# Matrix passes of 272, 256 and 264 columns in place of three of 264, on tiles whose blocks are 1152 or 1024 bytes apart

## The chip, the cores and the metric

One core of a Trainium2 chip runs the whole program; the other cores are idle. The metric is the device time of one execution in microseconds (us). Three executions of the kernel before took 2701.05, 2701.96 and 2702.11 us, median 2701.96.

## What is computed

One decoder layer for 256 prompt tokens and 8 decode tokens (one for each of 8 requests) that share the weights. In float32:

```
x = x + 1/2 * SwiGLU_1(RMSNorm(x))
h = RMSNorm(x);  one input projection h @ w_in
A = retention (8 heads; the prompt in chunks, the decode tokens from a state)
B = sparse attention (an indexer picks keys; 16 query heads, 4 key heads)
x = x + (sigmoid(g_A) * (A @ w_ret_out) + sigmoid(g_B) * (B @ w_att_out)) @ w_o
x = x + 1/2 * SwiGLU_2(RMSNorm(x))
```

The model width is 2048 and the FFN's 5632. All weights are read once, 512 KB for each half block of them. Nearly all arithmetic is in the products of the 264 tokens with the weights.

## The kernel before

The activations lie transposed: features on the 128 partitions, tokens along the columns, prompt tokens in columns 0 to 255 and decode tokens in 256 to 263 (T = TP + NB = 256 + 8). Sixteen blocks of 128 features make the model width.

Products with weights run on TensorE in a float32 form that reads rounded operands (F32R), so each operand is split into a rounded high part and the rest, the low part. `mblock` (L236) makes one output block of 128 features: it loads weights by SyncE's queue in two transfers of eight 128x128 blocks, rounds them on ScalarE (`wh`, L247), subtracts on VectorE or GpSimd (`wl`, L248), and for each 128 rows of the contraction runs three passes over all 264 tokens (below called a block of passes): `wh` with the high part (L251), `wh` with the low part (L252), `wl` with the high part (L253). Each pass is one weight load and one matmul, and all add into one PSUM tile `ps`; three such tiles exist. `Norm.add` (L280) and `split` (L301) make the high parts (ScalarE) and low parts (VectorE) of the activations.

High and low parts, x, and most other large tiles come from one pool, `qpool`, of NQ = 23 buffers of 4224 bytes a partition. `quad` (L146) takes a buffer, `Blocks` (L167) hands out its four blocks of 264 floats, 1056 bytes apart.

`ffn` (L305) runs in three chunks of the 5632 features: gate and up products, the SwiGLU product `h`, its split, then the second weight's products, added into x. Between the two FFNs stand the input projections (`mixblock`, one `mblock` each, in the order of L49: indexer, retention, attention, gates). Their evacuations are interleaved with generators that do everything else: `step` (L414) runs pieces of the queues a, b and c after each block, and `drain` empties them. Queue c holds `retention_prompt`, then `retention_decode` (L888: 16 steps, each takes three buffers, `sb`, `kq` and `kv`), then `group_norm` (L956). Queue b holds the decode indexer, then `decode_attention` (L786: eight requests in two half steps each; a request takes `kb`, a half step `qb` and two `pr`). Each half step's products run on GpSimd (L802, L905), the reductions on VectorE (L804, L906). The final order of each engine's instructions is found by the tile framework's scheduler from priorities; `ahead()` raises them. On each engine instructions run in that order.

The work on the path: `norm` and FFN1 (0 to 790 us), the projections with their generators (790 to 1640 us), the three output projections (to 1940 us), FFN2 (to the end).

Of the kernel before, what the change touches and what calls it, by code (L numbers as in the profile page):

```python
# [23 lines left out]
NB = 8  # L24
T = TP + NB
FF = 5632
FB = FF // P
# [23 lines left out]

NQ = 23
AHEAD = 1500
# [68 lines left out]
def layer(ctx: ExitStack, tc: tile.TileContext, xT, gains, consts, dmat, didx, pt, state, cidx, ck, cv,  # L122
# [22 lines left out]

    def quad(dt=F32, shape=(P, 4, T), s="q"):  # L146
        return qpool.tile(list(shape), dt, tag="q", name=nm(s))
# [19 lines left out]
    class Blocks:  # L167
# [3 lines left out]
        def __getitem__(self, i):  # L171
# [3 lines left out]
            return self.t[q][:, i % 4, :]  # L175

    warm = cpool.tile([P, 1], F32, name="warm")
    nc.vector.memset(warm, 0.0)
# [26 lines left out]
    nc.vector.memset(ones1, 1.0)  # L205
    onesw = cpool.tile([P, SW], F32, name="onesw")
    nc.vector.memset(onesw, 1.0)
# [27 lines left out]

    def mblock(src, nk, hi, lo, m=P):  # L236
        ps = psm.tile([P, 512], F32, tag="ps", name=nm("ps"))
        for c0 in range(0, nk, 8):
            n = min(8, nk - c0)
            wr = rawp.tile([P, 8, P], F32, tag="wr", name=nm("wr"))  # L240
            wh = hip.tile([P, 8, P], F32R, tag="wh", name=nm("wh"))
            wl = lop.tile([P, 8, P], F32R, tag="wl", name=nm("wl"))
            lo_turn[0] += 1
            eng = nc.gpsimd if lo_turn[0] % 4 in lo_pool[0] else nc.vector
            with ahead():
                nc.sync.dma_start(wr[:, :n, :m], src[:, c0:c0 + n, :])
                nc.scalar.activation(wh[:, :n, :m], wr[:, :n, :m], AF.Copy)  # L247
                eng.tensor_sub(wl[:, :n, :m], wr[:, :n, :m], wh[:, :n, :m])  # L248
            for k in range(n):
                g = c0 + k  # L250
                nc.tensor.matmul(ps[:m, :T], wh[:, k, :m], hi[g], start=g == 0, stop=False)  # L251
                nc.tensor.matmul(ps[:m, :T], wh[:, k, :m], lo[g], start=False, stop=False)  # L252
                nc.tensor.matmul(ps[:m, :T], wl[:, k, :m], hi[g], start=False, stop=g == nk - 1)  # L253
        return ps[:m, :T]
# [10 lines left out]
    def rsqrt(src, y, ms, t):  # L265
        """y = (src + EPS) ** -0.5"""
        nc.vector.tensor_scalar(ms, src, EPS, None, op0=ALU.add)
        root(ms, y, t)
        newton(y, ms, t)

    class Norm:
        """Gains and sums of squares of the blocks of x as they come; the mean's root follows at the evacuations."""

        def __init__(self, gain):
            self.gain = cc(gain)
            self.hi = Blocks(KB, F32R, "hi")
            self.lo = Blocks(KB, F32R, "lo")
            self.acc = wt("acc", tag="acc", bufs=2)

        def add(self, k, x):  # L280
            g = self.gain[:, k:k + 1]
            nc.scalar.activation(self.hi[k], x, AF.Copy, scale=g)  # L282
            nc.vector.scalar_tensor_tensor(self.lo[k], x, g, self.hi[k], op0=ALU.mult, op1=ALU.subtract)  # L283

# [15 lines left out]

    def split(v, hi, lo):  # L301
        nc.scalar.activation(hi, v, AF.Copy)
        nc.vector.tensor_sub(lo, v, hi)

    def ffn(norm, w1, w2, out, early=0):  # L305
        for ci, (j0, j1) in enumerate(CHUNKS):
            n = j1 - j0
            hh, hl = Blocks(n, F32R, "hh"), Blocks(n, F32R, "hl")
            for j in range(j0, j1):
                pg = mblock(w1[2 * j], KB, norm.hi, norm.lo)  # L310
                if j < early:
                    c = wt("c")
                    nc.scalar.activation(c, pg, AF.Copy)
                    pg = c
                if j == 0:
                    rstd = norm.done()
                g = wt("g")
                nc.vector.tensor_mul(g, pg, rstd)
                s = wt("s")
                nc.scalar.activation(s, g, AF.Silu)  # L320
                s2 = wt("s2")
                nc.gpsimd.tensor_mul(s2, s, rstd)  # L322
                pu = mblock(w1[2 * j + 1], KB, norm.hi, norm.lo)
                if j < early - 1:
                    c = wt("c")
                    nc.scalar.activation(c, pu, AF.Copy)
                    pu = c
                h = wt("h")
                nc.vector.tensor_mul(h, pu, s2)  # L329
                split(h, hh[j - j0], hl[j - j0])  # L330
            for m in range(KB):
                ps = mblock(w2[m][:, j0:j1, :], n, hh, hl)
                out(m, ps, ci == len(CHUNKS) - 1)
# [32 lines left out]
    def mixblock(src, m=P):  # L366
        return mblock(src, KB, mixn.hi, mixn.lo, m)

# [284 lines left out]
    def rms_roots(sums):  # L653
        """Steps from functions that give PSUM sums to the tiles of two roots each."""
        ss, y, t = (mt(n, (P, 2, T)) for n in ("ss", "y", "t"))
        for j, f in enumerate(sums):
            pq = aux()
            f(pq[:, :T])
            nc.scalar.activation(ss[:, j, :], pq[:, :T], AF.Identity, bias=epst)
        yield  # L660
        root(ss, y, t)
        yield
        newton(y, ss, t)
        yield y
# [210 lines left out]
    def bcast_rows(src, which, scale=1.0):  # L875
        """src [128 d, (b, h)] as rows of d in DRAM, to be read onto all partitions."""
        n = src.shape[1]
# [198 lines left out]
    lo_pool[0] = (0,)  # L1076
    RHI, RLO = Blocks(16, F32R, "rhi"), Blocks(16, F32R, "rlo")
    for i in range(16):
# [6 lines left out]
        nc.gpsimd.tensor_mul(r, s, RO[i])  # L1085
        split(r, RHI[i], RLO[i])
        step(b=1)
    drain("b")

    MG = Blocks(16, s="mg")  # L1090
    AHI, ALO = Blocks(16, F32R, "ahi"), Blocks(16, F32R, "alo")
    MHI, MLO = Blocks(16, F32R, "mhi"), Blocks(16, F32R, "mlo")

# [10 lines left out]
    for m in range(KB):  # L1104
        ps = mblock(wro[m], 16, RHI, RLO)
        nc.vector.tensor_mul(MG[m], ps, sgate(0, m))
        split(ATT[m], AHI[m], ALO[m])
    for m in range(KB):
        ps = mblock(wao[m], 16, AHI, ALO)
        t = wt("at")  # L1110
        nc.vector.tensor_mul(t, ps, sgate(1, m))
        t2 = wt("at2")
        nc.gpsimd.tensor_add(t2, t, MG[m])
        split(t2, MHI[m], MLO[m])

# [6 lines left out]
    for m in range(KB):  # L1122
        ps = mblock(wo[m], 16, MHI, MLO)
        nc.vector.tensor_add(X[m], ps, X[m])
# [79 lines left out]
```

## Time and profile before

| | us |
|---|---|
| median of three runs | 2701.96 |
| the profiled execution, its span from first to last instruction | 2703.1 |
| TensorE busy | 2621.5 (97%) |
| VectorE busy | 1596.6 (59%) |
| ScalarE busy | 1163.4 (43%) |
| GpSimd busy | 647.2 (24%) |

The profiled execution is known by its span alone. PE is TensorE, PEld its weight loads (which overlap the matmuls), DVE is VectorE, ACT ScalarE, POOL GpSimd, SP SyncE; a q behind a name is that engine's sequencer or its issue of a DMA. Matmuls are pipelined: the duration of one is its latency, and the time between the starts of two is what it costs. Names such as ps<-hi,wh say what an instruction writes and reads; L252 is line 252 of the kernel.

### The profile page before, as it was taken

How to read it: one execution, taken by the hardware profiler on the slowest of the kernel's cores; microseconds unless marked ns; L12 is line 12 of the kernel's file. 1: busy time of each engine (PE TensorE's matmuls, PEld its weight loads, DVE VectorE, ACT ScalarE, POOL GpSimd, SP SyncE). 2: the span in 40 equal slices, each digit the busy share in tenths (PEclk: the TensorE clock that was granted, in tenths of full speed). 3: DMA queues.
4: the chain of work that ended last, by engine and by line, in shares of the span. 5: the costliest groups of instructions: out<-in, count | busy, mean ns of one | idle time of the engine just before them, and what ended most of it. 6: DMA issues, size and time to landing. Idle time of an engine off the chain costs nothing.

```text
span 2703.1 us, 51188 instructions
## 1 busy us (share of the span) xinstructions
PE 2621.5 (97%) x21205; PEld 2588.8 (96%) x21205; DVE 1596.6 (59%) x2301; ACT 1163.4 (43%) x1551; POOL 647.2 (24%) x427
## 2 busy tenths in 40 slices
PE   7999999999999899999988899999999999999999
PEld 7999999999999699899988899999999999999999
DVE  6555555555566578568798845566655555554554
ACT  5443344334453333443545654444544334433443
POOL 3110011001127443445455543231111001100110
PEclk9999999999999899998998999999999999999999
DMA  6556555655566354468886666666555655566555
GB/s 216 180 181 184 181 180 181 184 182 180 173 218 214 108 170 157 141 213 282 266 291 228 203 195 223 206 208 210 180 181 182 181 183 180 180 181 183 181 166 173
DMA packets 164745, 520.67 MB, mean 193 GB/s; under 512 B 21680, under 2 KB 38640, under 8 KB 164512
## 3 DMA queue, kind: packets, MB, share of 16 engines
q1 hardware_dynamic: 126496, 445.31, 52.4%
q10 hardware_dynamic: 32112, 56.51, 6.4%
q0 software_dynamic: 5904, 15.59, 1.8%
q8 instruction: 166, 2.72, 0.4%
q14 instruction: 67, 0.55, 0.1%
HBM read 495.73 MB, written 21.60 MB: 191 GB/s over the span
## 4 chain that ended last, share of the span: by engine, by line
PE 82%; DVE 7%; issue 3%; DMA 3%; POOL 2%; ACT 2%; ACTq 0%; DVEq 0%; POOLq 0%
PE ps L252 27%; PE ps L251 26%; PE ps L253 26%; DVE wl L248 2%; DMA wr<-win 1%; POOL wl L248 1%; POOL pr L802 1%; DVE junk L534 1%; ACT wh L247 1%; DMA qb<-rows 0%; DMA kq<-rows 0%; DMA vb<-cv,rowi 0%; DVE sTs L804 0%; PE aux L443 0%; DVE sb L903 0%
## 5 line engine op out<-in xcount | busy, mean ns | idle before, releaser
L247 ACT ACTIVATE wh<-wr 128x1024 fp32r<-128x1024 f32 x866 | 902.0, 1043 | 1294.1 <-PE ps L252 838.5
L248 DVE TENSOR_TENSOR wl<-wr,wh 128x1024 fp32r<-128x1024 f32 (+2 forms) x798 | 990.3, 1241 | 740.2 <-ACT wh L247 739.1
L251 PE MATMUL ps<-hi,wh 128*128 128x264 f32 x4624 | 1326.4, 287 | 19.3 <-ACT hi L282 10.1
L253 PE MATMUL ps<-hi,wl 128*128 128x264 f32 x4624 | 1326.7, 287 | 16.2 <-DVE wl L248 13.3
L252 PE MATMUL ps<-lo,wh 128*128 128x264 f32 x4624 | 1329.2, 287 | 1.6 <-DVE lo L283 1.5
L251 PEld LDWEIGHTS ps<-hi,wh 128*128 128x128 f32 x4624 | 878.0, 190 | 23.0 <-ACT hi L282 10.1
L253 PEld LDWEIGHTS ps<-hi,wl 128*128 128x128 f32 x4624 | 876.1, 189 | 24.6 <-DVE wl L248 16.1
L252 PEld LDWEIGHTS ps<-lo,wh 128*128 128x128 f32 x4624 | 877.0, 190 | 8.7 <-issue 5.3
L322 POOL TENSOR_TENSOR s<-s,rstd 128x264 f32<-128x264 f32 x88 | 127.5, 1449 | 1252.6 <-ACT s L320 1252.6
L253 PE MATMUL ps<-hh,wl 128*128 128x264 f32 x1408 | 399.0, 283 | 0.0
L252 PE MATMUL ps<-hl,wh 128*128 128x264 f32 x1408 | 398.7, 283 | 0.0
L251 PE MATMUL ps<-hh,wh 128*128 128x264 f32 x1408 | 398.5, 283 | 0.0
L252 PEld LDWEIGHTS ps<-hl,wh 128*128 128x128 f32 x1408 | 264.7, 188 | 0.0
L251 PEld LDWEIGHTS ps<-hh,wh 128*128 128x128 f32 x1408 | 264.6, 188 | 0.0
L253 PEld LDWEIGHTS ps<-hh,wl 128*128 128x128 f32 x1408 | 264.4, 188 | 0.0
L248 POOL TENSOR_TENSOR wl<-wr,wh 128x1024 fp32r<-128x1024 f32 x68 | 170.2, 2508 | 289.9 <-ACT wh L247 250.4
L802 POOL TENSOR_TENSOR pr<-qb,kb 128x1024 f32<-128x1024 f32 x32 | 93.4, 2937 | 57.9 <-DMA qb<-rows 23.5
L291 POOL TENSOR_TENSOR acc<-acc,sq 128x264 f32<-128x264 f32 x45 | 40.5, 900 | 153.7 <-ACT sq L290 152.7
L329 DVE TENSOR_TENSOR h<-ps,s 128x264 f32<-128x264 f32 x88 | 38.0, 432 | 66.0 <-PE ps L253 62.7
L362 POOL DMA_INDIRECT kt<-cidx,kix x64 | 71.9, 1123 | 19.1 <-issue 18.5
L252 PE MATMUL ps<-mlo,wh 128*128 128x264 f32 x256 | 72.9, 285 | 0.0
L252 PE MATMUL ps<-alo,wh 128*128 128x264 f32 x256 | 72.7, 284 | 0.0
(311 smaller groups left out, 2270.0 us busy)
## 6 DMA issues: line engine op xcount, KB each, us to landing
wr<-win SPq DMA_DIRECT2D x224, 512.0 KB, 4.4
wr<-w1a SPq DMA_DIRECT2D x176, 512.0 KB, 3.8
wr<-w1b SPq DMA_DIRECT2D x176, 512.0 KB, 3.7
wr<-w2a SPq DMA_DIRECT2D x80, 512.0 KB, 3.7
wr<-w2b SPq DMA_DIRECT2D x80, 512.0 KB, 3.6
wr<-wro SPq DMA_DIRECT2D x32, 512.0 KB, 4.8
wr<-wao SPq DMA_DIRECT2D x32, 512.0 KB, 4.9
wr<-wo SPq DMA_DIRECT2D x32, 512.0 KB, 3.9
```

The lines of the kernel that those rows point to most:

```text
L247: nc.scalar.activation(wh[:, :n, :m], wr[:, :n, :m], AF.Copy)
L248: eng.tensor_sub(wl[:, :n, :m], wr[:, :n, :m], wh[:, :n, :m])
L251: nc.tensor.matmul(ps[:m, :T], wh[:, k, :m], hi[g], start=g == 0, stop=False)
L252: nc.tensor.matmul(ps[:m, :T], wh[:, k, :m], lo[g], start=False, stop=False)
L253: nc.tensor.matmul(ps[:m, :T], wl[:, k, :m], hi[g], start=False, stop=g == nk - 1)
L291: nc.gpsimd.tensor_add(self.acc, self.acc, sq)
L322: nc.gpsimd.tensor_mul(s2, s, rstd)
L329: nc.vector.tensor_mul(h, pu, s2)
L362: nc.gpsimd.indirect_dma_start(out=KT[p][pg // 8][:, o:o + PG], out_offset=None, in_=cidx, in_offset=bass.IndirectOffsetOnAxis(ap=kix[:, p ...
L534: nc.vector.scalar_tensor_tensor(junk, VS, thr, onesw, op0=ALU.is_ge, op1=ALU.mult, accum_out=out)
L802: nc.gpsimd.tensor_mul(pr, qb, k.to_broadcast([P, 2, 4, P]))
```

## The change

Three passes over 264, 264 and 264 columns become passes over 272, 256 and 264. The low parts of the eight decode tokens are stored right behind the high parts of all 264 tokens in the same block, so that the pass of `wh` over the wide block (272 columns, TW = T + NB) gives the high products of all tokens and, in eight more columns of PSUM, the low products of the decode tokens. The low parts of the prompt have a tile of their own, 256 floats a block. After the last pass ScalarE copies the eight extra columns out of PSUM, and VectorE adds them to columns 256 to 263.

```diff
-NQ = 23
+NQ = 21
+TW = T + NB
+TS = 288
...
+    class Pair:
...
+                self.t[q] = (qpool.tile([P, 4, TS], F32R, tag="q", name=nm(self.s + "h")),
+                             qpool.tile([P, 4, TP], F32R, tag="q", name=nm(self.s + "l")))
...
+        def hi(self, i):
+            return self.tiles(i)[0][:, i % 4, :T]
+        def wide(self, i):
+            return self.tiles(i)[0][:, i % 4, :TW]
+        def lod(self, i):
+            return self.tiles(i)[0][:, i % 4, T:TW]
+        def lop(self, i):
+            return self.tiles(i)[1][:, i % 4, :]
...
-                nc.tensor.matmul(ps[:m, :T], wh[:, k, :m], hi[g], start=g == 0, stop=False)
-                nc.tensor.matmul(ps[:m, :T], wh[:, k, :m], lo[g], start=False, stop=False)
-                nc.tensor.matmul(ps[:m, :T], wl[:, k, :m], hi[g], start=False, stop=g == nk - 1)
+                nc.tensor.matmul(ps[:m, :TW], wh[:, k, :m], x.wide(g), start=g == 0, stop=False)
+                nc.tensor.matmul(ps[:m, :TP], wh[:, k, :m], x.lop(g), start=False, stop=False)
+                nc.tensor.matmul(ps[:m, :T], wl[:, k, :m], x.hi(g), start=False, stop=g == nk - 1)
+        d = st([P, NB], tag="lod", bufs=4)
+        nc.scalar.activation(d[:m], ps[:m, T:TW], AF.Copy)
+        nc.vector.tensor_add(ps[:m, TP:T], ps[:m, TP:T], d[:m])
...
-    def split(v, hi, lo):
+    def split(v, x, i):
+        hi = x.hi(i)
         nc.scalar.activation(hi, v, AF.Copy)
-        nc.vector.tensor_sub(lo, v, hi)
+        for lo, c in ((x.lop(i), slice(0, TP)), (x.lod(i), slice(TP, T))):
+            nc.vector.tensor_sub(lo, v[:, c], hi[:, c])
```

`Norm.add` makes its low parts in the same two pieces. A buffer of the pool is now 4 x 288 floats, 4608 bytes; `quad` takes one of that size and gives views of 264 columns at a distance of 1152 bytes, so x, too, is loaded and stored in rows of 1056 bytes. The pool has 21 buffers. A constant, `onesw`, gets 16 more floats, which moves the pool behind it by 64 bytes: every block of the high and of the prompt's low parts now starts on a multiple of 128 bytes. In the kernel before, 1056 bytes being eight and a quarter times 128, one block in four did.

The order of each engine shows where the sizes and the new instructions stand. On TensorE, in the second chunk of FFN1, before (ps is the output block, hi and lo the norm's parts, wh and wl the weights'):

```order
L251 MATMUL ps_4268<-hi_138,wh_4270 128x264
L252 MATMUL ps_4268<-lo_140,wh_4270 128x264
L253 MATMUL ps_4268<-hi_138,wl_4271 128x264
L251 MATMUL ps_4268<-hi_148,wh_4300 128x264
L252 MATMUL ps_4268<-lo_150,wh_4300 128x264
L253 MATMUL ps_4268<-hi_148,wl_4301 128x264
```

and now (nh and nl are the norm's high and low tiles):

```order
L282 MATMUL ps_4493<-nh_142,wh_4495 128x272
L283 MATMUL ps_4493<-nl_143,wh_4495 128x256
L284 MATMUL ps_4493<-nh_142,wl_4496 128x264
L282 MATMUL ps_4493<-nh_156,wh_4525 128x272
L283 MATMUL ps_4493<-nl_157,wh_4525 128x256
L284 MATMUL ps_4493<-nh_156,wl_4526 128x264
```

The order is the same, and the columns differ.

On VectorE in the first chunk of FFN1, before (h is the SwiGLU product, hh and hl its parts, g the scaled gate):

```order
L329 TENSOR_TENSOR h_1814<-ps_1753,s_248_1751 128x264
L248 TENSOR_TENSOR wl_1918<-wr_1916,wh_1917 128x1024
L303 TENSOR_TENSOR hl_1419<-h_1814,hh_1418 128x264
L248 TENSOR_TENSOR wl_1955<-wr_1953,wh_1954 128x1024
L318 TENSOR_TENSOR g_1879<-ps_1818,rstd_282 128x264
```

and now:

```order
L287 TENSOR_TENSOR ps_1710<-ps_1710,lod_1771 128x8
L366 TENSOR_TENSOR h_1774<-ps_1710,s_251_1708 128x264
L279 TENSOR_TENSOR wl_1921<-wr_1919,wh_1920 128x1024
L340 TENSOR_TENSOR hl_1497<-h_1774,hh_1496 128x256
L340 TENSOR_TENSOR hh_1496<-h_1774,hh_1496 128x8
L279 TENSOR_TENSOR wl_1951<-wr_1949,wh_1950 128x1024
L287 TENSOR_TENSOR ps_1779<-ps_1779,lod_1840 128x8
L355 TENSOR_TENSOR g_1843<-ps_1779,rstd_301 128x264
```

Ahead of each reader of an output block stands the add of eight columns, and a split is two subtractions.

On GpSimd, among the gate projections, where retention_decode (kv) and decode_attention (pr) run, before:

```order
L802 TENSOR_TENSOR pr_14880<-qb_14878,kb_14875 128x1024
L802 TENSOR_TENSOR pr_14883<-qb_14878,kb_14875 128x1024
L802 TENSOR_TENSOR pr_15049<-qb_15047,kb_14875 128x1024
L905 TENSOR_TENSOR kv_14891<-sb_14886,kq_14888 128x1024
L802 TENSOR_TENSOR pr_15052<-qb_15047,kb_14875 128x1024
L782 DMA kb_15145<-ck,rowi_12896 128x512 x2
L802 TENSOR_TENSOR pr_15150<-qb_15148,kb_15145 128x1024
L905 TENSOR_TENSOR kv_15060<-sb_15055,kq_15057 128x1024
L802 TENSOR_TENSOR pr_15153<-qb_15148,kb_15145 128x1024
L905 TENSOR_TENSOR kv_15240<-sb_15235,kq_15237 128x1024
L802 TENSOR_TENSOR pr_15330<-qb_15328,kb_15145 128x1024
```

and now:

```order
L839 TENSOR_TENSOR pr_15571<-qb_15569,kb_15566 128x1024
L839 TENSOR_TENSOR pr_15574<-qb_15569,kb_15566 128x1024
L942 TENSOR_TENSOR kv_15582<-sb_15577,kq_15579 128x1024
L839 TENSOR_TENSOR pr_15746<-qb_15744,kb_15566 128x1024
L839 TENSOR_TENSOR pr_15749<-qb_15744,kb_15566 128x1024
L819 DMA kb_15845<-ck,rowi_13515 128x512 x2
L942 TENSOR_TENSOR kv_15757<-sb_15752,kq_15754 128x1024
L839 TENSOR_TENSOR pr_15850<-qb_15848,kb_15845 128x1024
L839 TENSOR_TENSOR pr_15853<-qb_15848,kb_15845 128x1024
L942 TENSOR_TENSOR kv_15943<-sb_15938,kq_15940 128x1024
L839 TENSOR_TENSOR pr_16036<-qb_16034,kb_15845 128x1024
```

Before, a product of the one stream stood between the two products of a half step of the other, and the next keys kb were gathered early; now a half step's two products stand together, and the streams take turns.

## Rows read from the trace of the kernel before

**Rows 1.** The page, part 1: busy us of each engine, share of the span, instructions.

```profile
PE 2621.5 (97%) x21205; PEld 2588.8 (96%) x21205; DVE 1596.6 (59%) x2301; ACT 1163.4 (43%) x1551; POOL 647.2 (24%) x427
```

**Rows 2.** The page, part 4: the chain of waits, shares by engine.

```profile
PE 82%; DVE 7%; issue 3%; DMA 3%; POOL 2%; ACT 2%; ACTq 0%; DVEq 0%; POOLq 0%
```

**Rows 3.** The page, part 5: passes on the two largest kinds of moving tile; busy us, mean ns.

```profile
L251 PE MATMUL ps<-hi,wh 128*128 128x264 f32 x4624 | 1326.4, 287 | 19.3 <-ACT hi L282 10.1
...
L251 PE MATMUL ps<-hh,wh 128*128 128x264 f32 x1408 | 398.5, 283 | 0.0
```

**Rows 4.** Busy time by stretch, FFN1 and FFN2: us, each engine (instructions), PEclk, DMA, GB/s.

```profile
50.00:150.00 100.00, 100.00 (x828) 100.00 (x827) 52.22 (x60) 42.21 (x52) 13.34 (x9) 1.00 0.59 184
...
2200.00:2400.00 200.00, 200.00 (x1647) 200.00 (x1647) 104.42 (x119) 82.18 (x101) 23.76 (x16) 1.00 0.57 181
```

**Rows 5.** Timeline of TensorE in FFN1, first passes of blocks: start us, us, instruction.

```profile
100.37 0.28 PE L251 MATMUL ps<-hi,wh 128*128 128x264 f32 x1
...
100.72 0.28 PE L251 MATMUL ps<-hi,wh 128*128 128x264 f32 x1
...
101.09 0.28 PE L251 MATMUL ps<-hi,wh 128*128 128x264 f32 x1
...
101.82 0.28 PE L251 MATMUL ps<-hi,wh 128*128 128x264 f32 x1
```

**Rows 6.** Busy time by stretch, after a wait of TensorE in the middle.

```profile
1459.00:1465.00 6.00, 6.00 (x29) 6.00 (x30) 6.00 (x10) 3.56 (x8) 0.01 (x1) 0.54 0.91 285
```

**Rows 7.** Timeline of TensorE there: first passes after the wait.

```profile
1458.91 0.59 PE L251 MATMUL ps<-hi,wh 128*128 128x264 f32 x1 [6.74 <-DVE g L984]
...
1459.52 0.42 PE L253 MATMUL ps<-hi,wl 128*128 128x264 f32 x1
1459.74 0.42 PE L251 MATMUL ps<-hi,wh 128*128 128x264 f32 x1
```

**Rows 8.** Timeline of TensorE in FFN2, first passes of blocks.

```profile
2050.15 0.28 PE L251 MATMUL ps<-hi,wh 128*128 128x264 f32 x1
...
2050.89 0.28 PE L251 MATMUL ps<-hi,wh 128*128 128x264 f32 x1
...
2051.61 0.28 PE L251 MATMUL ps<-hi,wh 128*128 128x264 f32 x1
```

**Rows 9.** Timeline of TensorE near the start: a wait and the passes behind it.

```profile
28.56 0.39 PE L252 MATMUL ps<-lo,wh 128*128 128x264 f32 x1 [1.54 <-DVE lo L283]
...
29.40 0.28 PE L252 MATMUL ps<-lo,wh 128*128 128x264 f32 x1
```

**Rows 10.** Groups by line and shape, VectorE and ScalarE: small instructions.

```profile
L861 DVE TENSOR_TENSOR ats<-aux,ow 128x8 f32<-128x8 f32 x16 | 1.4, 162 | 0.0
...
L1022 ACT ACTIVATE rvs<-rv 128x8 f32<-128x8 f32 x16 | 3.2, 198 | 12.2 <-DVE rv L1016 12.2
```

**Rows 11.** Timeline of ScalarE and VectorE: steps of the two decode streams.

```profile
1301.57 0.34 ACTq L894 DMA_DIRECT2D sb<-state  x1
...
1348.10 0.34 ACTq L894 DMA_DIRECT2D sb<-state  x1
...
1355.20 0.33 ACTq L798 DMA_DIRECT2D qb<-rows  x1
...
1363.04 1.22 DVE L906 TENSOR_REDUCE rd<-kv 128x8 f32<-128x1024 f32 x1 [2.31 <-POOL kv L905]
...
1368.75 1.22 DVE L804 TENSOR_REDUCE sTs<-pr 128x8 f32<-128x1024 f32 x1 [0.84 <-POOL pr L802]
...
1425.95 1.22 DVE L906 TENSOR_REDUCE rd<-kv 128x8 f32<-128x1024 f32 x1 [2.29 <-POOL kv L905]
```

**Rows 12.** Waits of TensorE, 1180 to 1600 us: the group norm's (us in total, times, longest).

```profile
PE aux L969 <- ACT sq L962: 2.1, 1, 2.1
```

**Rows 13.** Busy time by stretch, the gates with group norm and decode attention.

```profile
1400.00:1500.00 100.00, 84.22 (x603) 81.07 (x604) 92.25 (x106) 51.50 (x77) 59.99 (x26) 0.90 0.71 236
```

**Rows 14.** Timeline of ScalarE at the start.

```profile
9.54 1.74 ACT L282 ACTIVATE hi<-x,G 128x264 fp32r<-128x264 f32 x4 [3.89 <-DMA x<-xT]
```

More of the change, by code (lines that the diff above doesn't have):

```diff
@@ L144, in nm, with quad @@
         return f"{s}_{cnt[0]}"
-    def quad(dt=F32, shape=(P, 4, T), s="q"):
+    def quad(dt=F32, shape=None, s="q"):
+        if shape is None:
+            return qpool.tile([P, 4, TS], dt, tag="q", name=nm(s))[:, :, :T]
         return qpool.tile(list(shape), dt, tag="q", name=nm(s))
@@ L175, in __getitem__, with __init__, tiles @@
             return self.t[q][:, i % 4, :]
+    class Pair:
+        def __init__(self, n, s):
+            self.n, self.s, self.t = n, s, {}
+        def tiles(self, i):
+            q = i // 4
+            if q not in self.t:
+                self.t[q] = (qpool.tile([P, 4, TS], F32R, tag="q", name=nm(self.s + "h")),
+                             qpool.tile([P, 4, TP], F32R, tag="q", name=nm(self.s + "l")))
+            return self.t[q]
+        def hi(self, i):
[6 more added lines that the diff above has]
+            return self.tiles(i)[1][:, i % 4, :]
     warm = cpool.tile([P, 1], F32, name="warm")
@@ L205, in layer @@
     nc.vector.memset(ones1, 1.0)
-    onesw = cpool.tile([P, SW], F32, name="onesw")
+    onesw = cpool.tile([P, SW + 16], F32, name="onesw")[:, :SW]
     nc.vector.memset(onesw, 1.0)
@@ L234, in layer, with mblock @@
     lo_pool = [()]
-    def mblock(src, nk, hi, lo, m=P):
+    def mblock(src, nk, x, m=P):
         ps = psm.tile([P, 512], F32, tag="ps", name=nm("ps"))
@@ L275, in __init__ @@
             self.gain = cc(gain)
-            self.hi = Blocks(KB, F32R, "hi")
-            self.lo = Blocks(KB, F32R, "lo")
+            self.x = Pair(KB, "n")
             self.acc = wt("acc", tag="acc", bufs=2)
@@ L281, in add @@
             g = self.gain[:, k:k + 1]
-            nc.scalar.activation(self.hi[k], x, AF.Copy, scale=g)
-            nc.vector.scalar_tensor_tensor(self.lo[k], x, g, self.hi[k], op0=ALU.mult, op1=ALU.subtract)
+            hi = self.x.hi(k)
+            nc.scalar.activation(hi, x, AF.Copy, scale=g)
+            for lo, c in ((self.x.lop(k), slice(0, TP)), (self.x.lod(k), slice(TP, T))):
+                nc.vector.scalar_tensor_tensor(lo, x[:, c], g, hi[:, c], op0=ALU.mult, op1=ALU.subtract)
         def square(self, k, x):
@@ L307, in ffn @@
             n = j1 - j0
-            hh, hl = Blocks(n, F32R, "hh"), Blocks(n, F32R, "hl")
+            hx = Pair(n, "h")
             for j in range(j0, j1):
-                pg = mblock(w1[2 * j], KB, norm.hi, norm.lo)
+                pg = mblock(w1[2 * j], KB, norm.x)
                 if j < early:
@@ L322, in ffn @@
                 nc.gpsimd.tensor_mul(s2, s, rstd)
-                pu = mblock(w1[2 * j + 1], KB, norm.hi, norm.lo)
+                pu = mblock(w1[2 * j + 1], KB, norm.x)
                 if j < early - 1:
@@ L329, in ffn @@
                 nc.vector.tensor_mul(h, pu, s2)
-                split(h, hh[j - j0], hl[j - j0])
+                split(h, hx, j - j0)
             for m in range(KB):
-                ps = mblock(w2[m][:, j0:j1, :], n, hh, hl)
+                ps = mblock(w2[m][:, j0:j1, :], n, hx)
                 out(m, ps, ci == len(CHUNKS) - 1)
@@ L366, in mixblock @@
     def mixblock(src, m=P):
-        return mblock(src, KB, mixn.hi, mixn.lo, m)
+        return mblock(src, KB, mixn.x, m)
     blocks = {}
@@ L1076, in layer @@
     lo_pool[0] = (0,)
-    RHI, RLO = Blocks(16, F32R, "rhi"), Blocks(16, F32R, "rlo")
+    RX = Pair(16, "r")
     for i in range(16):
@@ L1085, in layer @@
         nc.gpsimd.tensor_mul(r, s, RO[i])
-        split(r, RHI[i], RLO[i])
+        split(r, RX, i)
         step(b=1)
@@ L1090, in layer @@
     MG = Blocks(16, s="mg")
-    AHI, ALO = Blocks(16, F32R, "ahi"), Blocks(16, F32R, "alo")
-    MHI, MLO = Blocks(16, F32R, "mhi"), Blocks(16, F32R, "mlo")
+    AXP, MXP = Pair(16, "a"), Pair(16, "m")
     def sgate(which, i):
@@ L1104, in layer @@
     for m in range(KB):
-        ps = mblock(wro[m], 16, RHI, RLO)
+        ps = mblock(wro[m], 16, RX)
         nc.vector.tensor_mul(MG[m], ps, sgate(0, m))
-        split(ATT[m], AHI[m], ALO[m])
+        split(ATT[m], AXP, m)
     for m in range(KB):
-        ps = mblock(wao[m], 16, AHI, ALO)
+        ps = mblock(wao[m], 16, AXP)
         t = wt("at")
@@ L1113, in layer @@
         nc.gpsimd.tensor_add(t2, t, MG[m])
-        split(t2, MHI[m], MLO[m])
+        split(t2, MXP, m)
     lo_pool[0] = ()
@@ L1122, in layer @@
     for m in range(KB):
-        ps = mblock(wo[m], 16, MHI, MLO)
+        ps = mblock(wo[m], 16, MXP)
         nc.vector.tensor_add(X[m], ps, X[m])
```

## Prediction

> **What bounds the kernel now.** Read the page's busy shares first [rows 1]: TensorE is busy 97% of a span of 2703.1 us, and the chain of waits [rows 2] is TensorE for 82%. Busy TensorE is not TensorE at its peak, so the next question is what one pass costs. The groups of instructions [rows 3] and the order give the number of passes: on each of three lines 4624 on norms' tiles, 1408 on the FFNs' products and 256 on each of three other pairs, 6800 in all, so 20,400 passes. Their mean of 287 ns is latency, since passes overlap; the spacing of their starts is what counts. Busy time by stretch [rows 4] has it: 828 instructions in 100 us of FFN1 are 120.8 ns each, 1647 in 200 us of FFN2 are 121.4. I use 121.1, the value between. So 20,400 passes are 2470 of the 2703 us.
>
> Why 121 and not fewer? At the lower level of the clock, 1.2 GHz (granted 0.54 on average over the stretch [rows 6]), after TensorE had waited 6.74 us [rows 7], successive passes start 0.22 us apart: 264 columns at that level are 220.0 ns, nothing over. At 2.4 GHz the columns alone would be 110.0 ns. The 11 ns above that are not in the array; something that does not speed up with its clock feeds it. The timeline of FFN1 [rows 5] says more: a block (three passes) starts at 100.37, 100.72, 101.09, and the third and fourth end at 101.82. So the first took 0.35 us, the next 0.37, the last two 0.73, and the next four read the same. Blocks stand 1056 bytes apart, eight and a quarter times 128, so of four only one starts on a multiple of 128 (the third of a tile, as the pool lies at an odd multiple of 64; the change adds 16 floats before it). The short one is that one: 116.7 ns a pass against 121.7 to 123.3.
>
> **The change, part by part.** *Pass length.* 272 + 256 + 264 = 3 x 264: no column is saved. What changes is where passes start and how many bytes they touch. Two estimates, one answer. (a) All blocks become like the aligned one: 116.7 ns. (b) A piece of 128 bytes is 32 columns, 13.33 ns at 2.4 GHz; 1056 bytes touch nine pieces wherever they start on a multiple of 32 bytes: 120.0 ns, 1.1 below what is measured. The new passes touch 9, 8 and 9: 26 pieces for three, 115.6 ns, plus the same 1.1: 116.7. Bounds: no pass can be shorter than its columns, 110.0 ns on average; none of the rows has a block longer than 0.37 us, 123.3 ns a pass, which would be a loss of 2.2. Between these I take 116.7, the row that is the same thing (an aligned start), 4.4 ns less per pass; the range needs 115.6 (no surplus over the pieces) on one side and 121.1 (nothing gained) on the other. That all blocks turn as long as the longest has no mechanism here, since each new start is of the kind that is short today.
>
> The Trainium skill's page "TensorE: Matmul & The Clock Gate", section "Back-to-back issue gap", has the gap of warm matmuls as columns over 2.4 plus 2.5 ns, with no word of the address. By it the sum of three passes would stay as it is and this term would be 0; it would also make today's pass 112.5 ns, which [rows 4] contradict with 121.
>
> *Where the gain lands.* The two FFNs and the output projections (50 to 850 and 1600 to 2703 us) run TensorE without a gap [rows 4]: at 121 ns the first 800 us hold about 6,600 passes, and the last 1103 us 9,100. Together 15,700, times 4.4 ns: **-69 us**. The first part of the middle (850 to 1285 us) holds 48 blocks of output of 48 passes, by TensorE's order: 2,300 passes, 10 us, of which I take **-7**, since TensorE idles there for other engines. From 1285 to 1433 us I take nothing (next term). From 1433 to 1600, 20 output blocks, 970 passes, 4 us: **-2**, as VectorE is busy 92% there [rows 13].
>
> *The pool.* 23 buffers become 21. While gates are computed, the code holds up to 18 (8 of the norm, 4 ro, kg, vn, 4 qn), so 5 were left for two streams and 3 remain, more as qn tiles go. A retention-decode step wants three (sb, kq, kv), a half step of decode attention four (kb, qb, two pr). In the order of GpSimd above they were interleaved; now each step stands whole behind the other. A retention step lasts from 1348.10 to 1364.26, 16.2 us, a half step from 1355.20 to 1369.97, 14.8 us [rows 11]. Overlapped, six of the one and seven of the other took from 1301.6 to 1427 us, 21 us a pair. One after the other a pair is 31, less some 3 to 5 where a buffer comes free before its step ends: 5 to 6 more for each of five pairs. Who waits: the group norm's first matmul stands in TensorE's order behind the 218th output block whatever the streams do, and it already waited 2.1 us for them [rows 12], so there is no slack: **+25**. Bounds: 0 (alone, each step gets its transfers and VectorE sooner) and +55 (five pairs at 31).
>
> *VectorE and ScalarE.* Each block's evacuation gains a 128x8 copy by ScalarE, 0.198 us by the nearest row, and a 128x8 add by VectorE, 0.162 us [rows 10]; each split gains a 128x8 subtraction. 433 blocks make 70 us of VectorE and 86 of ScalarE, 184 splits another 30. In the FFNs this lies beside passes: a block takes 5.8 us, three PSUM buffers leave two blocks for its evacuation, and VectorE is half idle. The cover is gone between 1285 and 1600 us: 41 blocks x 0.162 = 6.6, I take **+5** (bounds 0, 13).
>
> *Start and end.* The first wide pass needs the low parts too, one VectorE step, and x's rows land in pieces of 1056 bytes rather than 4224; ScalarE now waits 3.89 us for x [rows 14]: **+2** (bounds 0 and +4, that wait doubled). The last block's evacuation is 0.36 us longer: **+0.4**.
>
> Sum: -69 - 7 - 2 + 25 + 5 + 2 + 0.4 = -45.6. The profiled execution's 2703.1 becomes 2657.5; it stands 1.1 us above the runs' median of 2701.96, so **2656 us**. With passes of 116.0 to 117.8 ns and 5 to 50 us for the pool the forecast's own range is 2625 to 2695.
>
> **The rivals.** *Better on both counts* (14%): passes at 115.6 ns and streams that catch up: 15,700 x 5.5 = 86, 10 in the middle, less 7.4: 2613. For it: 120.0 is near a floor that few stretches exceed by more than 1.8. Against: the 2.1 us of [rows 12].
>
> *Half the gain* (13%). In FFN2 [rows 8] the blocks from 2050.15 to 2051.61 took 0.74 and 0.72 by twos, no 0.35 among four, though one of four is aligned there too; what differs is where high and low tiles lie to each other. If the start counts only for some pairs, 2.2 ns a pass: -34 - 4 + 32 = 2696.
>
> *Slower: the pass is not set by reading but by feeding two instructions each* (a weight load and a matmul), which no address changes: every pass stays at 121 ns, and what is left is the pool, the small instructions and the start: 2703 + 32 - 1 = **2734**. It decides as soon as the gain is under 2.0 ns a pass (32 us over 15,700). For it: 121 holds in every stage, nearly whatever the tiles. Against: behind a wait of 1.54 us, in which a queue would fill, six starts still take 0.84 us [rows 9], no faster; and the 0.35 blocks. 13%. The same page, section "Wait — 56ns, not 53.3ns?", has the sequencer at about 62 ns a matmul when instructions are not decoded in hardware; two of them would be an estimate of 124 ns, near the 121 here, and the address would not matter. The 0.35 us blocks lie under it, so the trace bears it out poorly.
>
> *The change doesn't do what it says*: the built order shows passes of 272, 256 and 264, so only the sizes' effect is open (2%).
>
> **How the numbers follow.** Forecast 58%, better 14%, half 13%, feed 13%, other 2%. A measurement of this kernel can tell 0.2%, 5.4 us, from no change. Faster: 56 of the forecast's 58 (the rest is a pool cost over 60), 14, and 6 of the half: 76%. Same: 6%. Slower: 13 of the feed, 3 of the half, 2: 18%. The range 2610 to 2712 leaves out the feed case and little more.
>
> **What would show it.** Right: all blocks 0.35 us in both FFNs; some 857 instructions in 100 us of FFN1; the group norm's matmul after a wait of tens of us, with retention steps and half steps of decode attention in turn; VectorE some 100 us busier. Wrong: block times that still differ by place or tile (half the gain), 0.36 to 0.37 everywhere (feed), no wait at the group norm (then 2630), or passes of 256 columns no shorter than those of 272.

## The result, and the profile after

The changed kernel took 2740.83 us (median of 4 runs, 2739.36 to 2747.98), the kernel before 2702.03 beside it (4 runs): a ratio of 1.0147, interval 1.0132 to 1.0163. It is 39 us slower, where 46 us less was forecast. The profiled executions span 2740.0 and 2703.1 us, 36.9 apart, and the working below is against that.

The page's busy row of the changed kernel; its instruction counts answer to [rows 1].

```profile
PE 2626.5 (96%) x21205; PEld 2595.4 (95%) x21205; DVE 1657.0 (60%) x2918; ACT 1192.5 (44%) x1988; POOL 647.6 (24%) x427
```

TensorE is busy 5 us longer, where 78 us less were forecast; VectorE is 60 us busier, where some 100 were. Busy time by stretch (us, each engine with its instructions, PEclk, DMA share, GB/s), same columns as [rows 4] and [rows 13]:

```profile
50.00:150.00 100.00, 100.00 (x824) 100.00 (x823) 55.14 (x89) 43.04 (x69) 11.87 (x8) 1.00 0.60 184
1400.00:1500.00 100.00, 70.30 (x495) 67.00 (x496) 85.45 (x106) 46.74 (x86) 59.87 (x27) 0.88 0.72 237
2200.00:2400.00 200.00, 200.00 (x1647) 200.00 (x1646) 107.11 (x163) 82.06 (x127) 19.24 (x13) 1.00 0.56 181
```

824 instructions in 100 us of FFN1 where 828 stood and 857 were forecast; 1647 in 200 us of FFN2, as before. In the middle 495 in place of 603. The blocks of FFN1 in TensorE's timeline (start, duration, instruction), against [rows 5]:

```profile
100.04 0.29 PE L282 MATMUL ps<-nh,wh 128*128 128x272 f32 x1
100.16 0.28 PE L283 MATMUL ps<-nl,wh 128*128 128x256 f32 x1
100.28 0.29 PE L284 MATMUL ps<-nh,wl 128*128 128x264 f32 x1
100.41 0.29 PE L282 MATMUL ps<-nh,wh 128*128 128x272 f32 x1
...
100.77 0.29 PE L282 MATMUL ps<-nh,wh 128*128 128x272 f32 x1
...
101.13 0.29 PE L282 MATMUL ps<-nh,wh 128*128 128x272 f32 x1
```

Every block now takes 0.36 to 0.37 us: 121.7 ns a pass. The 0.35 of one block in four is gone, not spread. Over 6,001 passes of 50 to 780 us the start of the next lies on average 125.6 ns behind one of 272 columns, 117.0 behind one of 256 and 122.4 behind one of 264, though single intervals of one size scatter (112 to 122 ns for 256). The averages go with the columns, and the mean of all is 121.66, against 121.1 before.

TensorE's waits (us in total, times, longest) where the decode streams run:

```profile
PE aux L1006 <- ACT sq L999: 17.7, 1, 17.7
PE ps L284 <- DVE wl L279: 15.7, 11, 4.8
PE ps L282 <- DVE g L1021: 14.5, 5, 5.3
```

The group norm's matmul (L1006) waits 17.7 us where it waited 2.1 [rows 12]. ScalarE's timeline there shows for what:

```profile
1454.44 0.34 ACTq L945 DMA_DIRECT2D o_sts<-sb  x1
1459.95 0.34 ACTq L931 DMA_DIRECT2D sb<-state  x1
1460.34 1.36 ACT L999 ACTIVATE sq<-ro 128x264 f32<-128x264 f32 x4 [12.04 <-DVE ro L948]
```

The square reads the copy of retention decode's results (L948), so it stands behind that stream's 15th step, the last one that works on the first four of the eight heads. Since both programs run the same 20,400 passes in almost the same order, the start of the same pass in both traces says where the time came in (us, differences taken before rounding):

| pass | before | after | later by | gained or lost since | forecast |
|---|---|---|---|---|---|
| 600 | 93.8 | 96.8 | 2.9 | +2.9 | +2, and 3 of -69 |
| 6,600 | 820.9 | 827.9 | 7.0 | +4.1 | of -69, 26 |
| 9,600 | 1297.8 | 1301.7 | 3.9 | -3.1 | -7 |
| 11,400 | 1606.2 | 1639.8 | 33.5 | +29.7 | +25 + 5 - 2 |
| 20,399 | 2699.5 | 2735.9 | 36.4 | +2.9 | of -69, 40 |
| end | 2703.1 | 2740.0 | 36.9 | +0.5 | +0.4 |

In sum the pool, the small instructions, the start and the end came about as forecast. One term is missing whole: the shorter passes, 69 us where TensorE has no gaps and the 7 and 2 of the middle (the 3.1 gained there come without them: with 21 buffers and passes as before it is 2.5).

### The profile page after: what moved, and what is told of

The parts are those of the page before. It is cut to its first block, busy times and chain, and to the rows that moved or that the text cites. A ratio compares the mean times of both kernels' runs of the same rounds, so it can differ in the third digit from the quotient of the medians.

```text
span 2740.0 us, 52569 instructions
## 1 busy us (share of the span) xinstructions
PE 2626.5 (96%) x21205; PEld 2595.4 (95%) x21205; DVE 1657.0 (60%) x2918; ACT 1192.5 (44%) x1988; POOL 647.6 (24%) x427
## 5 line engine op out<-in xcount | busy, mean ns | idle before, releaser
L282 PE MATMUL ps<-nh,wh 128*128 128x272 f32 x4624 | 1353.7, 293 | 32.2 <-DVE g L1021 14.5
L284 PE MATMUL ps<-nh,wl 128*128 128x264 f32 x4624 | 1336.6, 289 | 24.8 <-DVE wl L279 21.0
L283 PE MATMUL ps<-nl,wh 128*128 128x256 f32 x4624 | 1309.3, 283 | 0.0
L282 PEld LDWEIGHTS ps<-nh,wh 128*128 128x128 f32 x4624 | 881.3, 191 | 40.7 <-issue 21.7
L284 PEld LDWEIGHTS ps<-nh,wl 128*128 128x128 f32 x4624 | 880.5, 190 | 30.5 <-DVE wl L279 24.6
L283 PEld LDWEIGHTS ps<-nl,wh 128*128 128x128 f32 x4624 | 884.5, 191 | 3.2 <-issue 2.6
L282 PE MATMUL ps<-hh,wh 128*128 128x272 f32 x1408 | 405.8, 289 | 0.0
L283 PE MATMUL ps<-hl,wh 128*128 128x256 f32 x1408 | 393.6, 280 | 0.0
L282 PE MATMUL ps<-ah,wh 128*128 128x272 f32 x256 | 73.9, 289 | 0.0
L282 PE MATMUL ps<-rh,wh 128*128 128x272 f32 x256 | 73.9, 289 | 0.0
```

The source lines that it names most:

```text
L282: nc.tensor.matmul(ps[:m, :TW], wh[:, k, :m], x.wide(g), start=g == 0, stop=False)
L283: nc.tensor.matmul(ps[:m, :TP], wh[:, k, :m], x.lop(g), start=False, stop=False)
L284: nc.tensor.matmul(ps[:m, :T], wl[:, k, :m], x.hi(g), start=False, stop=g == nk - 1)
```

## The experiments

Two questions: why the aligned passes are not shorter, and what makes up the 29.7 us of the middle. The comparisons below give medians, ratios to the kernel before on the same chip with a 95% interval (worked out over the single executions, so not quite the quotient of the medians), and for the middle the time from the 9,600th to the 11,400th pass against before's 308.4 us. The middle is known from one trace of each kernel. Three of the whole kernels ran on two chips where the kernel before, too, took longer: the exchanged passes and 21 buffers without the copy and the add on one (before 2737 us), 1280 bytes on another (2747). Their profiles show TensorE waiting for its own issue some 30 us around 900 us, so only ratios and other stretches are used.

**Passes alone.** Two kernels of nothing but rows of passes on constant tiles; the core of the first:

```diff
+        for i in range(n):
+            x = passes[i % len(passes)]
+            N = x.shape[-1]
+            k = 0 if one_w else (i // 3 % 8)
+            nc.tensor.matmul(ps[:m, :N], w[:, k, :m], x, start=each or i == 0, stop=each or i == n - 1)
```

> A kernel of passes alone (the layer is left out): rows of 240 passes on constant tiles, first with the other engines idle, then beside loads, ScalarE copies and VectorE subtractions of weights. Theory 1, columns at a rate: the spacing of passes goes with the columns and not with addresses: 121 ns for 264 columns on 1056-byte blocks and on aligned blocks alike (within 1 ns), 117 for 256, 146 for 320, 234 for 512 if it is a rate of 0.457 ns a column, or 144 and 224 if it is the columns at 2.4 GHz plus 11 ns; the same pass beside other engines within 1 ns. Theory 2, feeding two instructions: 121 ns for 256 as for 264, then 133 for 320 and 213 for 512, no surplus over the columns. Theory 3, address (the forecast's): 116 to 117 on aligned blocks and on one aligned block read over and over, 120 to 123 on an odd start. Theory 4, the other engines' reads and writes: about 112 while they are idle, 121 beside them. Half the weight columns or one weight block for all passes: no change by theories 1, 3 and 4.

Busy time by stretch of the first kernel, each within one row of passes: blocks 1152 bytes apart; 272/256/264 columns on 1152 and 1024; 256 columns; 384; 512; one aligned block over and over; bf16; plain float32; and blocks 1152 apart again, beside loads, ScalarE and VectorE.

```profile
82.00:110.00 28.00, 28.00 (x233) 28.00 (x232) 0.00 (x0) 0.00 (x0) 0.00 (x0) 1.00 0.00 1
111.00:139.00 28.00, 28.00 (x233) 28.00 (x232) 0.00 (x0) 0.00 (x0) 0.00 (x0) 1.00 0.00 1
140.00:168.00 28.00, 28.00 (x238) 28.00 (x237) 0.00 (x0) 0.00 (x0) 0.00 (x0) 1.00 0.01 1
204.00:244.00 40.00, 40.00 (x233) 40.00 (x232) 0.00 (x0) 0.00 (x0) 0.00 (x0) 1.00 0.00 1
246.00:299.00 53.00, 53.00 (x236) 43.85 (x235) 0.00 (x0) 0.00 (x0) 0.00 (x0) 1.00 0.00 1
300.00:328.00 28.00, 28.00 (x235) 28.00 (x234) 0.00 (x0) 0.00 (x0) 0.00 (x0) 1.00 0.00 1
358.00:384.00 26.00, 26.00 (x234) 22.61 (x232) 0.00 (x0) 0.00 (x0) 0.00 (x0) 1.00 0.00 1
473.00:525.00 52.00, 52.00 (x235) 44.42 (x234) 0.00 (x0) 0.00 (x0) 0.00 (x0) 1.00 0.00 1
584.00:613.00 29.00, 29.00 (x241) 29.00 (x240) 18.45 (x16) 16.31 (x16) 0.00 (x0) 1.00 0.80 279
```

A stretch also counts the two or so passes under way when it begins, so the spacing is better taken from the first and last start of a row (ns):

| row | spacing | columns at 2.4 GHz | over |
|---|---|---|---|
| 264, blocks 1056 apart from 64 past a multiple of 128 | 122.8 | 110.0 | 12.8 |
| 264, blocks 1152 apart, aligned; the same beside other engines | 121.7; 121.6 | 110.0 | 11.7 |
| 272, 256, 264, aligned as in the change | 121.65 | 110.0 | 11.65 |
| 264, one aligned block | 120.0 | 110.0 | 10.0 |
| 256 | 118.9 | 106.7 | 12.2 |
| 320; 384; 512 | 146.7; 173.3; 226.8 | 133.3; 160.0; 213.3 | 13.3; 13.3; 13.5 |
| 264 in bf16 | 112.5 | 110.0 | 2.5 |
| 264 in plain float32 (220.0 is two cycles a column) | 222.5 | 220.0 | 2.5 |

Theory 1 holds in the main: a pass of this format costs its columns and a gap of 10 to 13.5 ns. Of its two forms the columns plus a gap fits (226.8 at 512, not 234), but the gap is no constant 11: 256 columns take 118.9, not 117, and 512 take 226.8, not 224. Blocks 1056 and 1152 bytes apart differ by 1.1 ns, a little over the 1 that it allows, and half the weight columns bring 119.9 where it expected no change; one weight block for all passes brings none (122.7). Theory 2, feeding, falls: 320 columns take 146.7, not 133, and the gap does not shrink where there is time to feed; the bf16 row has as many instructions and 2.5 ns (both operands change format there, so the rows do not say which of them brings the gap). Theory 3 falls: aligned blocks take 121.7, not 117. Theory 4 falls: the other engines change nothing here.

> Passes alone again (the layer is left out), rows of 192 on constant tiles with the other engines idle; names tell the distance of blocks and of low from high tiles in floats, the start of a single block, the number of weight columns or of moving columns. Theory 1 (columns plus a gap): 264 columns take 120 to 123 ns in every layout and order, none under 119; 256, 258, 260, 272 and 288 columns rise by 0.42 ns a column on average. If some layout is what made the short blocks (aligned, with low tiles an odd multiple of 128 bytes away): that row at 116 to 118. If the gap is the weight load's: 96, 64 and 32 weight columns take steadily less, to below 118 for 32.

The second kernel tried fifteen layouts, another order and other sizes. Stretches of five rows: 1056 apart from 64 past a multiple; 1056 apart from a multiple; 1152 apart; 1280 apart; 288 columns.

```profile
46.00:69.00 23.00, 23.00 (x190) 23.00 (x189) 0.00 (x0) 0.00 (x0) 0.00 (x0) 1.00 0.01 1
140.00:162.00 22.00, 22.00 (x184) 22.00 (x183) 0.00 (x0) 0.00 (x0) 0.00 (x0) 1.00 0.01 1
326.00:348.00 22.00, 22.00 (x183) 22.00 (x182) 0.00 (x0) 0.00 (x0) 0.00 (x0) 1.00 0.01 1
443.00:465.00 22.00, 22.00 (x186) 22.00 (x185) 0.00 (x0) 0.00 (x0) 0.00 (x0) 1.00 0.00 1
747.00:771.00 24.00, 24.00 (x182) 24.00 (x181) 0.00 (x0) 0.00 (x0) 0.00 (x0) 1.00 0.01 1
```

By first and last starts they take 122.8, 121.1, 121.6, 120.0 and 133.2 ns. All layouts lie between 120.0 and 123.1, none at 117: the address counts for some 3 ns, but not as the forecast had it; reading the high block twice in a row gives 121.7 on two of them. 256, 258, 260, 264, 272 and 288 columns take 118.9, 120.9, 120.0, 121.6, 126.1 and 133.2: 0.45 ns a column over the whole. 96, 64 and 32 weight columns (122.8 with 128) take 121.4, 119.4 and 120.0: some 3 ns of the gap go with them, not steadily, and never below 118.

The second kernel also has the short block, and not where the forecast would put it. With blocks 1056 bytes apart from a multiple of 128, the four blocks of a tile take 366, 365, 352 and 371 ns, before's pattern in FFN1 (366, 366, 351, 371); here the short third one starts 64 bytes past a multiple. With the starts that before's tiles have, from 64 past, where the third block is the aligned one, they take 372, 367, 367 and 368 in the first kernel.

**Alignment in the layer.**

```diff
-NQ = 23
+NQ = 21
...
+            return qpool.tile([P, 4, 288], dt, tag="q", name=nm(s))[:, :, :T]
...
+    onesw = cpool.tile([P, SW + 16], F32, name="onesw")[:, :SW]
```

> The kernel before with blocks 1152 bytes apart, all on multiples of 128 bytes, three passes of 264 columns, 21 buffers, no extra instructions. Theory 1 (columns): passes at 121 to 122 ns as before, and the pool's 22 to 32 us: 2724 to 2740. Theory 3 (aligned starts help, and only the mixed lengths or the distance of low to high blocks spoil it): 116 to 118 ns a pass, about 60 us less, 2660 to 2680.

It took 2732.9 us, 1.0100 (1.0076 to 1.0125). From the 600th to the 6,600th pass its trace needs 730.5 us, as the changed kernel's 731.2, before's 727.1: three aligned passes of 264 cost what 272, 256 and 264 cost, and 0.5 ns a pass more than unaligned. So neither the mixed lengths nor anything added beside them spoils a gain; there is none. And with every block on a multiple of 128 bytes the blocks of a tile still differ. The first passes of five successive blocks in its FFN1:

```profile
100.22 0.29 PE L253 MATMUL ps<-hi,wh 128*128 128x264 f32 x1
...
100.59 0.29 PE L253 MATMUL ps<-hi,wh 128*128 128x264 f32 x1
...
100.96 0.28 PE L253 MATMUL ps<-hi,wh 128*128 128x264 f32 x1
...
101.32 0.28 PE L253 MATMUL ps<-hi,wh 128*128 128x264 f32 x1
...
101.68 0.29 PE L253 MATMUL ps<-hi,wh 128*128 128x264 f32 x1
```

On average over 60 to 350 us the four take 371, 370, 359 and 359 ns. A short block in a pattern of twelve passes is no sign of an aligned start.

**The pool alone.**

```diff
-NQ = 23
+NQ = 21
```

> The kernel before with a pool of 21 buffers in place of 23 and nothing else. If the pool costs the middle its time: 22 to 32 us slower than before (2724 to 2734), TensorE waiting 15 us or more at the group norm's first matmul, passes still at 121 ns. If it was the small instructions of VectorE and ScalarE or the split subtractions: within 5 us of before.

2725.53 us against 2707.22, 1.0079 (1.0054 to 1.0103), the middle 20.8 us longer: the pool, if a little under the 22 to 32 of the forecast. Its group norm waits 12.8 us, not 15:

```profile
PE aux L969 <- ACT sq L962: 12.8, 1, 12.8
```

Passes stay at 121.1 ns. VectorE's reductions at the ends of the 10th to the 15th retention step show the pace up to the step that the group norm waits for (durations, first and last start; before, with 21 buffers, and of the changed kernel):

```profile
L906 DVE TENSOR_REDUCE rd<-kv x6: 1204/1206/1223, 1331.1 to 1426.0; 128x8 f32<-128x1024 f32 x6
```

```profile
L906 DVE TENSOR_REDUCE rd<-kv x6: 1203/1208/1222, 1333.7 to 1446.1; 128x8 f32<-128x1024 f32 x6
```

```profile
L943 DVE TENSOR_REDUCE rd<-kv x6: 1203/1213/1221, 1339.8 to 1456.9; 128x8 f32<-128x1024 f32 x6
```

Five steps take 94.9, 112.4 and 117.1 us. Each is 3.5 and 4.4 us longer, a little under the 5 to 6 of the forecast. The pace differs between programs anyway: the seven here with 23 or 24 buffers take 94.6 to 110.3 us for these steps, the four with 21 take 112.4 to 117.1. The group norm's wait has 10.7 of the 20.8 us; the rest is the balance of other waits, of which that for the weights' low part grew most (8.5 to 21.7 us between 1340 and 1660).

**Buffers and small instructions, apart and together.** The changed kernel with 23 buffers fits if its blocks are 272 floats apart:

```diff
-TS = 288
+TS = 272
...
-NQ = 21
+NQ = 23
```

> The changed kernel with high blocks 272 floats apart (1088 bytes, so half of them start 64 bytes past a multiple of 128) and 23 buffers. If the pool holds the 28 us of the middle and the alignment nothing: 2708 to 2716, passes at 121 to 122 ns, wait at the group norm under 8 us. If the small instructions of the evacuations hold it: 2730 to 2742. If the alignment were worth something that the pool hides: above 2740.

2723.52 us against 2707.22, 1.0061 (1.0039 to 1.0083): 16 us over its before, where the change is 39 over its own and the pool alone was expected to leave 6 to 14. The group norm waits 8.5 us, a little over the 8. Passes take 121.7 ns, as in the change, though only half of the high blocks are aligned.

The same without the copy and the add (they are the evacuation's three lines in the change's diff):

> The changed kernel with 23 buffers (high blocks 272 floats apart) and without the copy and the add of an evacuation, so the low parts of the decode tokens are left out of the products. If the small instructions hold 8 to 16 us: 2707 to 2715, against 2722 with them. If they do not: within 4 us of 2722.

2714.56 us against 2704.59, 1.0030 (1.0019 to 1.0041): some 8 us less than with them, inside the range for the small instructions. The group norm's wait is before's again:

```profile
PE aux L1003 <- ACT sq L996: 2.1, 1, 2.1
```

And with 21 buffers, without them:

> The changed kernel with its 21 buffers, without the copy and the add of an evacuation (the low parts of the decode tokens are left out of the products). If the 9 us that they cost at 23 buffers add to the pool's price: 2728 to 2734. If with 21 buffers they lie under the wait for the streams: 2737 to 2742.

1.0123 (1.0079 to 1.0167), too wide to choose. The trace leans to the second: the middle is 27.4 us longer, the wait 12.1.

| middle, longer by (us) | 21 buffers | 23 buffers |
|---|---|---|
| with copy and add | 29.7 (the change) | 14.1 |
| without | 27.4 | 5.5 |

So the pool costs 15.6 to 22.0 us, and the small instructions 8.6 with 23 buffers but 2.3 with 21, as if there they lay under the wait for the streams. That they do is argued, not shown: each entry is one trace of one order, and the runs below move the middle by -4 to +7 us where buffers are not short.

Do small instructions cost that much by themselves? The kernel before with a copy and an add of zeros at each evacuation, and with the add alone:

```diff
+        d = st([P, NB], tag="lod", bufs=4)
+        nc.scalar.activation(d[:m], ps[:m, :NB], AF.Copy, scale=0.0)
+        nc.vector.tensor_add(ps[:m, TP:T], ps[:m, TP:T], d[:m])
```

> The kernel before, 23 buffers and three passes of 264, with the evacuation's two small instructions alone: behind every output block ScalarE makes eight columns of zeros from PSUM and VectorE adds them to columns 256 to 263 (the result does not change). If these two hold what the pool does not (the 19 us that stay when 23 buffers are given back, less 6 of passes and start): 8 to 16 us slower, TensorE waiting 5 to 10 us at the group norm. If they lie beside other work: within 4 us of before, and the rest of the middle belongs to the order that the scheduler finds or to the split subtractions.

> The same with VectorE's add alone, of a constant tile of zeros, and no copy by ScalarE. If VectorE's time (433 adds of 0.167 us, some 10 us between 1285 and 1600 us) is the price: as with both, 7 to 14 us. If it is the chain copy, then add, ahead of each evacuation: under 4 us.

With both 2704.11 against 2704.59, 0.9997 (0.9986 to 1.0007): nothing, although the trace has 433 adds of 167 ns and copies of 157. The group norm waits 7.5 us there, the middle is 1.2 longer. With the add alone 2713.15, 1.0027 (1.0016 to 1.0039), 7 us more, though less work is added; in its trace the middle is 4.1 us shorter, and 8.7 us had come in between the 6,600th and the 8,400th pass. Both theories of the add fail: it has no price of its own that holds from one program to the next. What is left is the order that the scheduler finds for each program; no run tests that by itself.

**More buffers, another order of passes, fewer buffers.**

```diff
-NQ = 23
+NQ = 24
```

> The kernel before with 24 buffers in place of 23. If the pool still binds at 23: 4 to 12 us faster than before. If 23 were enough, and only 21 too few: within 4 us. Passes at 121 ns either way.

2704.99 against 2704.59, 0.9997 (0.9987 to 1.0008): 23 were enough. The middle is 6.7 us longer in its one trace, though nothing was taken away: a measure of that scatter.

```diff
-                nc.tensor.matmul(ps[:m, :T], wh[:, k, :m], lo[g], start=False, stop=False)
-                nc.tensor.matmul(ps[:m, :T], wl[:, k, :m], hi[g], start=False, stop=g == nk - 1)
+                nc.tensor.matmul(ps[:m, :T], wl[:, k, :m], hi[g], start=False, stop=False)
+                nc.tensor.matmul(ps[:m, :T], wh[:, k, :m], lo[g], start=False, stop=g == nk - 1)
```

> The kernel before with the second and third pass exchanged (high, high, low in place of high, low, high), so the same block is read twice in a row. By theory 1 within 4 us of before, passes at 121 ns. If the address of the pass ahead matters (one block over and over took 120.0 ns): up to 10 us faster in the stages without gaps, against a third pass that now waits for the weights' low part a little earlier.

2757.77 us against 2737.50, 1.0065 (1.0041 to 1.0089): slower, which neither expectation had. Its FFN1 has fewer instructions in 100 us than before's 828 [rows 4]:

```profile
50.00:150.00 100.00, 100.00 (x821) 100.00 (x820) 51.78 (x59) 41.40 (x51) 13.38 (x9) 1.00 0.58 184
```

From starts a pass takes 122.1 ns there and 121.8 in FFN2, where before had 121.1 and 121.5. Alone, the same order was 1.1 ns faster than high, low, high on the same blocks (121.7 against 122.8, and in the layer before's order on these starts takes 121.1): rows alone carry over to the layer to one or two nanoseconds, not below.

```diff
-NQ = 21
+NQ = 20
...
-            return qpool.tile([P, 4, 288], dt, tag="q", name=nm(s))[:, :, :T]
+            return qpool.tile([P, 4, 320], dt, tag="q", name=nm(s))[:, :, :T]
```

> The kernel before with blocks 1280 bytes apart (multiples of 128 and of 1280, the layout of the row alone that took 119.97 ns) and only 20 buffers. If that row holds beside the layer: 119.8 to 120.3 ns a pass, 857 or fewer but at least 831 passes in 100 us of both FFNs, 15 to 25 us less over the program, against a pool that costs 25 to 45 in the middle: 2705 to 2730 on a chip where before takes 2702 to 2707. If the layer's weights and traffic wipe it out: 121 to 122 ns and 2730 to 2750.

(The diff is against the aligned kernel above.) 2838.79 us against 2746.77, 1.0328 (1.0304 to 1.0353): both expectations missed. Passes in both FFNs take 121.3 ns; only the three output projections run at the row's 120.0. And one buffer fewer costs 72 us more than 21 did on aligned blocks: the middle is 97.5 us longer, against 25.5, with this wait:

```profile
PE aux L971 <- ACT sq L964: 78.1, 1, 78.1
```

The five steps take 110.3 us there, no longer than with 21; but the stream is late by then, as this row of the view above shows (1445.1 in place of 1331.1, of which some 42 us had come in before the middle):

```profile
L908 DVE TENSOR_REDUCE rd<-kv x6: 1208/1221/1223, 1445.1 to 1555.4; 128x8 f32<-128x1024 f32 x6
```

No version tried beats the kernel before.

## Why the prediction was wrong

**Pass length (-69, measured +7, the 4.1 and 2.9 of the table): the step that failed.** "All blocks become like the aligned one: 116.7 ns" took the interval between two starts for the price of the pass between them. In before's FFN1 [rows 5] four blocks took 0.35, 0.37 and twice 0.36 to 0.37 us, 1.45 together, 121.1 ns a pass: what the aligned block gained its neighbours lost. It was not short for its start, either: with all four blocks aligned two are still shorter than the others (371, 370, 359, 359 ns), and alone the same short block stands 64 bytes past a multiple. Make every block aligned and the mean of the row is 121.7. Estimate (b), 26 pieces of 128 bytes for 27, came out at the same 116.7 by chance; that a pass is priced by such pieces was assumed, and with 26 pieces the changed passes take what 27 take (121.65 and 121.7 alone). The bounds I drew from single blocks (116.7, 123.3) were bounds on a share, not on a sum; the right one was in the trace, since 1056-byte blocks in four different positions summed to 1.45 us each time. That passes might become longer I excluded, and was wrong by half a nanosecond: aligned blocks take 121.7 in both FFNs, against 121.1 and 121.5. Why is open: the kernel with only half of its high blocks aligned takes 121.7 too, and alone blocks with before's own starts take more than aligned ones (122.8 against 121.7), only those from a multiple of 128 less (121.1).

The observation at the lower clock stands. With 1.2 GHz granted there is nothing over the columns, now too. Busy time and TensorE's timeline of the changed kernel near the start:

```profile
20.10:24.80 4.70, 4.70 (x21) 4.70 (x22) 4.70 (x10) 4.70 (x14) 4.39 (x5) 0.50 0.42 153
```

```profile
20.46 0.42 PE L283 MATMUL ps<-nl,wh 128*128 128x256 f32 x1
20.67 0.42 PE L284 MATMUL ps<-nh,wl 128*128 128x264 f32 x1
20.89 0.43 PE L282 MATMUL ps<-nh,wh 128*128 128x272 f32 x1
21.12 0.42 PE L283 MATMUL ps<-nl,wh 128*128 128x256 f32 x1
```

The granted clock is 0.50, and three passes of 792 columns take 0.66 us, which is 792 at 1.2 GHz. But that the gap vanishes there does not show what feeds the array, nor that the gap depends on the address. What the gap is made of stays open; shown is that it comes with this operand format (2.5 ns in bf16), per pass, and that the total of columns sets the rest.

The Trainium skill's "TensorE: Matmul & The Clock Gate", section "Back-to-back issue gap", has a matmul's isolated gap, as it calls it, cost the columns and a constant, without the address. In that form it was right, and by it the term was 0. Its constant, 2.5 ns, is what the bf16 and the plain float32 row show; for this kernel's format the rows show 10 to 13.5.

**The pool (+25, measured 15.6 to 22): about right.** With two buffers fewer the steps take longer, 3.5 to 4.4 us each over five where I said 5 to 6, and the group norm behind the 15th step has no slack. That I put all of it on that one wait was wrong; it has about half. That 20 buffers would cost 97.5 I had not seen.

**Small instructions (+5, measured 2.3 beside the pool's wait): not decided.** That the sum with the pool came to 29.7 against 28 is in part luck: in other programs the same instructions cost 8.6 us or nothing, a scatter that no term of mine had.

**Start (+2) and end (+0.4): right**, 1.6 at the first pass and 2.9 by the 600th, then 0.5.

**The slower rival (2734) named the time but not the reason.** Its "every pass stays at 121" held; its feeding of two instructions did not: 512 columns keep the gap that feeding would hide, and passes of 256, 264 and 272 columns differ about as their columns do. The section "Wait — 56ns, not 53.3ns?" of the same page, by which I estimated 124 ns, is not what limits here, since the bf16 row issues as many instructions at 112.5. The rival got 13% where the evidence against it was one wait's six starts and the 0.35 us blocks. The second was no evidence. The other two rivals fell with the forecast: no row and no stage has three such passes at a mean of 115.6 ns, and places of tiles move a pass by up to 3 ns, but none of fifteen brings it under 120.0.

## What to carry to other kernels

Price a pipelined instruction by the length of a whole repeating pattern (here twelve passes), never by the shortest interval in it; before rebuilding a layout on one such interval, time that layout alone, in a kernel of passes. Moving columns between passes saved nothing while their sum stayed: count columns and passes. And where a pool is cut to make room for padding, look for the stream whose steps hold several buffers and for who waits at its end; the price can grow steeply, here in the middle 0 at 24 and 23 buffers within the scatter, 21 us at 21, 97 at 20 (that one with another layout, too).

## What was not expected of the hardware

The gap between passes of rounded float32 is four to over five times that of bf16 or plain float32 (10 to 13.5 against 2.5 ns in all rows of 128 weight columns but one), and is absent at 1.2 GHz. The exception is one block read over and over: it takes 120.0, 122.2, 120.9 or 126.6 ns when it starts 0, 32, 64 or 96 bytes past a multiple of 128. Passes of 320, 384 and 512 columns come at 11, 13 and 17 times 13.33 ns, to the nanosecond. In the kernel with blocks 1280 bytes apart one layout takes 120.0 ns a pass in the output projections and 121.3 in the FFNs, and no run says why. And on two chips the kernel before took 35 to 45 us longer than on the others; the three kernels profiled there had TensorE wait some 30 us for its own issue, which no profile of the other chips shows.
